# Score matmuls of a head pair in one batch, later side pieces, and a last gate strip finished by token tile

## The chip, the cores and the metric

The kernel runs on one core of a Trainium2 chip. The metric is the device time of one execution in microseconds (us), as the median of repeated runs. One further execution was recorded by the hardware profiler; every row below comes from that one.

## The reference

A two-layer encoder trunk over 256 tokens with a model width of 2048. Layer 0 mixes tokens by windowed grouped-query attention (32 query heads of 64, 4 key heads, a sink logit per head), layer 1 by differential attention (8 heads, each with two softmax maps of width 128). Each layer goes on with a gated feed-forward of width 5632 and with an embedding that is added through a gate.

```python
for i in range(DEPTH):
    hn = rms_norm(h, attn_norm[i])
    mix = windowed_gqa_sink(...) if i % 2 == 0 else diff_attention(...)
    h = h + mix
    h = h + swiglu(rms_norm(h, ffn_norm[i]), w_ffn_in[i], w_ffn_out[i])
    gate = sigmoid(rms_norm(h, ple_gate_norm[i]) @ ple_w_gate[i])
    h = h + rms_norm(p[i] @ ple_w_proj[i], ple_post_norm[i]) * gate

# layer 0: sc = q k^T * 64**-0.5 - slope * |t-s|, masked to |t-s| <= 128, softmax with the sink
# layer 1: sc = q k^T * 128**-0.5 - slope * |t-s|; probs[0] - lam * probs[1]; then v, rms_norm
```

## The kernel before

All 256 tokens stay on the chip as two token tiles (NM = 2) of 128. Every large product is cut into column strips of 512 (W). A strip is a `Group`: it runs over the contraction in steps k of 128 rows, and at each step over both token tiles, with three matmuls each, because both operands are held as a high and a low part (hi x hi, lo x hi, hi x lo). Such a matmul, 128x512 out, is called a strip matmul here (line 161 before, line 176 after, since the change shifts the lines). There are 9600 of them. The weights come by DMA into `raw`, and for every two steps k ScalarE (ACT) makes the high part `ws` and VectorE (DVE) the low part.

Everything else on TensorE (PE) is cut into side pieces, which are put between strip matmuls. PE's order is written by the kernel itself. `Flow` keeps a heap of pieces with due times on a clock `now`, which each strip matmul moves on by MM = 0.23. `flow.later(delay, fn)` enters a piece that is due `delay` after the present value of the clock; after each strip matmul `flow.tick` runs one step of the piece at hand, up to its next `yield`. So a piece that yields after each of its matmuls has a strip matmul between each two of them. Where a strip needs something that a piece has yet to make (`flow.until`), the pieces are run without strip matmuls in between; this is called a drain here. The order on ACT, DVE and GpSimd (POOL) is the scheduler's, and each of those engines works its list in that order.

The pieces of layer 0: `to_q` turns queries to columns by four transposes (line 386); `heads` makes the scores of two heads (line 396, helper `scores`) and sends them through `exps` (DVE `sc` and `nm`, ACT `e`, then POOL); `turn` transposes the weights of the two heads (line 425, eight transposes, then the splits `wT`); `weigh` multiplies them with the values (line 509, twelve matmuls, then the split of the result, `xt`). There are 16 head pairs. A score matmul of layer 0 contracts over 64 rows, one head on rows 0 to 63 and the other on rows 64 to 127 of the array. When one of the four strips of queries ends, `qk_norm` makes squares on ACT, sums `ss` on DVE, a reciprocal root in seven steps on POOL (its result is `rr`), and the normed queries `qn` on DVE.

Layer 1 has the same pieces with other sizes: the scores of a map are six matmuls over 128 rows, two maps for each of eight heads, and they read the keys and queries `qk` that `turn_side` splits on ACT and DVE just before. `Norm.turn` transposes the residual `h` (line 257) for the next product. All side pieces write into one pool of four buffers of the accumulation memory (`at`), taken in turn, so a piece waits until the fourth buffer back has been read.

The last strip of the whole program is the fourth gate strip of layer 1: after its last matmul, `gated` makes the sigmoid on ACT (line 727), two products and sums on DVE (lines 728 and 730), and one output DMA for each token tile (line 732).

Of the kernel before, what the change touches and what calls it, by code (L numbers as in the profile page):

```python
# [12 lines left out]
F32 = mybir.dt.float32  # L13
F32R = mybir.dt.float32r
AF = mybir.ActivationFunctionType
ALU = mybir.AluOpType
AX = mybir.AxisListType

P = 128
T = 256  # L20
NM = T // P
D = 2048
KT = D // P
W = 2 * T
SK = W // P
NS = D // W
# [9 lines left out]
MM = 0.23  # L36
# [49 lines left out]
def encoder(ctx: ExitStack, tc: tile.TileContext, x, p, attn_norm, ffn_norm, a_w_qkv, a_q_norm,  # L86
# [3 lines left out]
    nc = tc.nc  # L90
# [32 lines left out]
    def mslice(m):  # L123
        return slice(m * P, (m + 1) * P)
# [17 lines left out]
    class Group:  # L142


        def __init__(self, w, r0, n, c, xs, done, before=None):
            self.w, self.r0, self.n, self.c, self.xs, self.done, self.before = w, r0, n, c, xs, done, before
            self.blocks = [(b, min(4, n - b)) for b in range(0, n, 4)]

        def run(self, feed):
            if self.before:  # L150
                self.before()
            ps = [mm_ps() for _ in range(NM)]
            for k in range(self.n):
                if k % 2 == 0:
                    ws = feed.next()
                flow.until(lambda: len(self.xs) > k)
                x, hi, lo = self.xs[k], ws[:, 0, k % 2, :], ws[:, 1, k % 2, :]
                for m in range(NM):
                    c = mslice(m)
                    for i, (a, w) in enumerate(((0, hi), (1, hi), (0, lo))):  # L160
                        nc.tensor.matmul(ps[m], x[:, a, c], w, start=(k == 0 and i == 0),  # L161
                                         stop=(k == self.n - 1 and i == 2))
                        flow.tick(MM)
            self.ps = ps
            if self.done:
                self.done(ps)

    class Feed:

# [71 lines left out]
    class Norm:  # L241
# [2 lines left out]
        def __init__(self, col):  # L244
            self.col, self.stat, self.xs = col, Stat(), Slots()

        def add(self, s):
            self.stat.add([h[:, m, s * W:(s + 1) * W] for m in range(NM)])
            for k in range(s * SK, (s + 1) * SK, 2):
                flow.later(2.0, lambda k=k: self.turn(k))  # L250

        def turn(self, k):

# [136 lines left out]
    def scores(heads):  # L390

        for m in range(NM):
            c = mslice(m)
            for i, (a, b) in enumerate(((0, 1), (1, 0), (0, 0))):
                for ps, q, k in heads:
                    nc.tensor.matmul(ps[:, m, :], q[:, a, c], k[:, b, :], start=(i == 0), stop=(i == 2))  # L396
                yield 0.12 * len(heads)

    def exps(ps, d, slope, ap, extra=None):

# [40 lines left out]
    class AttentionA:  # L441
# [52 lines left out]
        def turn(self, j, es):  # L494
            wts = []
            for e in es:
                yield from keys_first(e, self.ap, WT_BUFS, wts)
                busy["e"] -= 1
            flow.later(2.0, lambda: self.weigh(j, wts))

        def weigh(self, j, wts):
            ps = at_ps()[:, 0, :]
# [19 lines left out]
    class AttentionB:  # L522
# [16 lines left out]
        def turn_side(self, hd, which, toks, b):  # L539
            s = self.hd.setdefault(hd, {"e": {}})  # L540
            t = self.ap.tile([P, 2, 2, T], F32R, name=f"qk{which}", tag=f"qk{which}", bufs=2)
            yield from to_pairs(t, toks, b * T, (gq_b, gk_b)[which])
            s[which] = t
            if which == 1:
                for c in range(2):
                    flow.later(2.0 + 2.0 * c, lambda c=c: self.scores(hd, c))

        def values(self, s):
            def done(ps):
# [81 lines left out]
    def project(w, os, norm):  # L631

        def done(half, s):
            def add(ps):
                add_to_h(ps, s)
                if half == 1:
                    norm.add(s)
            return add
        n = KT // 2

        class Half:
            def __len__(self):
                return max(0, len(os) - n)

            def __getitem__(self, k):
                return os[n + k]
        return [Group(w, half * n * P, n, s, (os, Half())[half], done(half, s))
                for half in range(2) for s in range(NS)]

    class FeedForward:  # L650
# [64 lines left out]
        def out(self, s, last):  # L715
            def done(ps):
                add_to_h(ps, s)
                if last:
                    self.gate.add(s)
            return done  # L720

        def gated(self, s, nxt):
            def done(ps):
                c = slice(s * W, (s + 1) * W)
                for m in range(NM):
                    g = self.fp.tile([P, W], F32, name="gate", tag="gate", bufs=2)
                    nc.scalar.activation(out=g, in_=ps[m], func=AF.Sigmoid, scale=self.gate.stat.col(m))
                    nc.vector.scalar_tensor_tensor(out=g, in0=g, scalar=self.pstat.col(m), in1=self.pe[:, m, c],  # L728
                                                   op0=ALU.mult, op1=ALU.mult)
                    nc.vector.tensor_tensor(out=h[:, m, c], in0=h[:, m, c], in1=g, op=ALU.add)  # L730
                    if nxt is None:
                        nc.sync.dma_start(out=out[mslice(m), c], in_=h[:, m, c])
                if nxt is not None:
                    nxt.add(s)
            return done

        def groups(self, nxt):
            lay, first, out, w_in = self.layer, 0, [], w_ffn_in[self.layer]
            for part in PARTS:
                last = first + part == FF // P  # L740
                hs = Slots()
                for i in range(part // SK):
                    s = first // SK + i
                    out.append(Group(w_in, 0, KT, s, self.norm.xs, self.gate_in))
                    out.append(Group(w_in, 0, KT, FF // W + s, self.norm.xs, self.up(hs, i * SK)))
                    if s < NS:
                        out.append(Group(ple_w_proj[lay], 0, 2, s, self.pp, self.embed(s)))
                for s in range(NS):
                    out.append(Group(w_ffn_out[lay], first * P, part, s, hs, self.out(s, last)))
                first += part  # L750
            out[0].before = self.start
            return out + [Group(ple_w_gate[lay], 0, KT, s, self.gate.xs, self.gated(s, nxt)) for s in range(NS)]

    attn_a = AttentionA(norm_a)
    norm = Norm(C_FFN)
# [25 lines left out]
    with tc.manual_schedule(engines={mybir.EngineType.Activation, mybir.EngineType.DVE}):  # L781
        for q in range(2):
            for _ in put_x(q):
                pass
        flow.later(6 * MM, lambda: put_x(2))
        flow.later(24 * MM, lambda: put_x(3))
        groups[0].done, first_done = None, groups[0].done
        groups[0].run(feed)
        for q in range(NS):
            feed.split()  # L790
            norm_a.stat.add([h[:, m, q * W:(q + 1) * W] for m in range(NM)])
    feed.ahead = WS_BUFS
    first_done(groups[0].ps)
    flow.later(3.0, small_vectors)
    for g in groups[1:]:
        g.run(feed)
# [53 lines left out]
```

## Time and profile before

| | us |
|---|---|
| median of 3 runs | 2399.95 |
| the 3 runs | 2399.94, 2399.95, 2404.16 |
| time of the profiled execution | 2401.06 |
| its span, first to last instruction | 2399.3 |
| PE busy in the span | 2367.5 |

The span is 1.8 us less than the time of that execution. Three views are read: the groups of instructions (busy time, count, mean), the timeline of an engine (start, length, what it waited for), and the sums over stretches. The end of a matmul is modelled in this profile, so what a matmul costs is read from start to start, not from its length. A bracket in a timeline row gives the idle time ahead of it and the engine that ended it.

### The profile page before, as it was taken

To read this page: it belongs to the slowest core of one execution; us is meant where nothing else is said; L and a number is where in the kernel's file an instruction comes from. 1 tells how busy PE (TensorE), PEld (TensorE's weight loads), DVE (VectorE), ACT (ScalarE), POOL (GpSimd) and SP (SyncE) were. 2 spreads that over 40 slices of the span, in tenths; PEclk is the share of its full clock that TensorE was granted. 3 is DMA by queue.
4 is the path that set the end of the run, shared out by engine and by line. 5 is a ranking of instruction groups with operands and counts; after the bars stand their busy time and mean duration, and the time that the engine had idled before them with its cause. 6 is when DMAs were issued, how large, how long until landed. Compare 5 with 4: busy or idle time off the path is not lost.

```text
span 2399.3 us, 28442 instructions
## 1 busy us (share of the span) xinstructions
PE 2367.5 (99%) x10853; PEld 1924.6 (80%) x10853; DVE 1345.4 (56%) x1546; ACT 1112.9 (46%) x1549; POOL 137.9 (6%) x309
## 2 busy tenths in 40 slices
PE   8999999999999999999999999999999999999998
PEld 6776788888888888887877888888888888888887
DVE  5667655555454454565557566655545554454564
ACT  5455454434434444455455454554444434434453
POOL 1232000000000000000111211000000000000000
PEclk9999999999999999999999999999999999999999
DMA  6432355555555555555544544555555555555553
GB/s 231 143 106 88 137 181 193 187 193 185 193 193 193 190 187 195 187 179 174 192 155 161 176 158 148 210 186 197 185 184 199 187 193 193 191 191 194 178 196 138
DMA packets 121281, 428.71 MB, mean 179 GB/s; under 512 B 13520, under 2 KB 16184, under 8 KB 120888
## 3 DMA queue, kind: packets, MB, share of 16 engines
q1 hardware_dynamic: 121144, 426.89, 51.0%
q8 instruction: 85, 1.39, 0.2%
q14 instruction: 52, 0.43, 0.0%
HBM read 424.74 MB, written 2.10 MB: 178 GB/s over the span
## 4 chain that ended last, share of the span: by engine, by line
PE 90%; DVE 2%; ACT 1%; issue 0%; POOL 0%; DVEq 0%; ACTq 0%; POOLq 0%
PE mm L161 86%; PE at L396 1%; PE at L708 1%; PE at L257 1%; DVE ws L139 1%; PE at L509 1%; PE at L595 0%; ACT ws L138 0%; PE at L425 0%; ACT e L411 0%; DVE gate L728 0%; PE at L386 0%; DVE qk L199 0%; DVE nm L407 0%; DVE sc L405 0%
## 5 line engine op out<-in xcount | busy, mean ns | idle before, releaser
L161 PE MATMUL mm<-ws,xt 128*128 128x512 f32 x9600 | 2324.8, 397 | 2.2 <-ACT xt L194 0.9
L161 PEld LDWEIGHTS mm<-ws,xt 128*128 128x128 f32 x9600 | 1790.1, 188 | 405.3 <-ACT xt L194 1.8
L139 DVE TENSOR_TENSOR ws<-raw,ws 128x1024 fp32r<-128x1024 f32 x800 | 978.1, 1226 | 875.5 <-ACT ws L138 875.0
L138 ACT CAST ws<-raw 128x1024 fp32r<-128x1024 f32 x800 | 840.6, 1052 | 1047.4 <-PE mm L161 958.8
L205 POOL TENSOR_SCALAR rs_v<-ssum 128x2 f32<-128x2 f32 x8 | 1.5, 193 | 1714.4 <-DVE ssum L234 1714.4
L286 DVE TENSOR_TENSOR h<-mm,h 128x512 f32<-128x512 f32 x96 | 62.0, 681 | 3.9 <-PE mm L161 3.9
L411 ACT ACTIVATE e<-sc,nm 128x257 f32<-128x257 f32 (+1 forms) x96 | 47.9, 501 | 34.6 <-DVE nm L407 34.3
L257 PE MATMUL at<-ident,h 128*128 128x128 f32 x192 | 52.7, 288 | 8.2 <-DMA h<-in_x_dram 6.0
L198 ACT ACTIVATE xt<-at,gains 128x256 fp32r<-128x256 f32 x96 | 43.2, 474 | 34.5 <-DVE xt L199 33.8
L194 ACT CAST xt<-at 128x256 fp32r<-128x256 f32 x108 | 37.9, 372 | 43.1 <-DVE xt L195 31.8
L199 DVE SCALAR_TENSOR_TENSOR xt<-at,gains,xt 128x256 fp32r<-128x256 f32 x96 | 44.1, 479 | 17.8 <-ACT xt L198 17.8
L195 DVE TENSOR_TENSOR xt<-at,xt 128x256 fp32r<-128x256 f32 x108 | 43.3, 418 | 15.6 <-ACT xt L194 15.3
L509 PE MATMUL at<-wT,vp 128*128 128x256 f32 x192 | 48.5, 291 | 2.8 <-DVE wT L195 2.0
L708 PE MATMUL at<-ident,hid 128*128 128x128 f32 x176 | 47.8, 272 | 0.0
L207 POOL TENSOR_TENSOR rs_y<-rs_v,halves 128x2 f32<-128x2 f32 (+2 forms) x29 | 44.8, 1546 | 2.4
L376 DVE TENSOR_TENSOR qn<-mm,rr 128x512 f32<-128x512 f32 (+1 forms) x28 | 16.9, 647 | 44.0 <-POOL rr L366 44.0
L425 PE MATMUL at<-ident,e 128*128 128x128 f32 x160 | 40.2, 272 | 0.8 <-DVE sc L405 0.8
L405 DVE SCALAR_TENSOR_TENSOR sc<-dist,at 128x512 f32<-128x512 f32 x48 | 31.5, 682 | 16.2 <-PE at L396 16.2
L689 ACT ACTIVATE silu<-mm,rinv 128x512 f32<-128x512 f32 x44 | 29.9, 688 | 19.7 <-PE mm L161 19.7
L257 PEld LDWEIGHTS at<-ident,h 128*128 128x128 f32 x192 | 27.7, 148 | 13.9 <-DMA h<-in_x_dram 6.6
L509 PEld LDWEIGHTS at<-wT,vp 128*128 128x128 f32 x192 | 34.2, 197 | 4.2 <-DVE wT L195 2.5
L396 PEld LDWEIGHTS at<-kd,qT 64*128 64x128 f32 x192 | 17.7, 183 | 24.3 <-issue 17.8
(90 smaller groups left out, 698.3 us busy)
## 6 DMA issues: line engine op xcount, KB each, us to landing
raw<-in_w_ffn_in_dram SPq DMA_DIRECT2D x352, 512.0 KB
raw<-in_w_ffn_out_dram SPq DMA_DIRECT2D x176, 512.0 KB
raw<-in_b_w_qkv_dram SPq DMA_DIRECT2D x96, 512.0 KB
raw<-in_ple_w_gate_dram SPq DMA_DIRECT2D x64, 512.0 KB
raw<-in_a_w_qkv_dram SPq DMA_DIRECT2D x40, 512.0 KB
raw<-in_a_w_o_dram SPq DMA_DIRECT2D x32, 512.0 KB
raw<-in_b_w_o_dram SPq DMA_DIRECT2D x32, 512.0 KB
raw<-in_ple_w_proj_dram SPq DMA_DIRECT2D x16, 256.0 KB
```

The lines of the kernel that those rows point to most:

```text
L138: nc.scalar.copy(out=ws[:, 0], in_=src)
L139: nc.vector.tensor_tensor(out=ws[:, 1], in0=src, in1=ws[:, 0].bitcast(F32), op=ALU.subtract)
L161: nc.tensor.matmul(ps[m], x[:, a, c], w, start=(k == 0 and i == 0), stop=(k == self.n - 1 and i == 2))
L195: nc.vector.tensor_tensor(out=lo, in0=src, in1=hi.bitcast(F32), op=ALU.subtract)
L198: nc.scalar.activation(out=hi, in_=src, func=AF.Copy, scale=scale)
L199: nc.vector.scalar_tensor_tensor(out=lo, in0=src, scalar=scale, in1=hi.bitcast(F32), op0=ALU.mult, op1=ALU.subtract)
L207: nc.gpsimd.tensor_tensor(out=y, in0=v, in1=halves[:, :n], op=ALU.pow)
L257: nc.tensor.transpose(ps[:, j, mslice(m)], h[:, m, (k + j) * P:(k + j + 1) * P], ident)
L286: nc.vector.tensor_tensor(out=hs, in0=ps[m], in1=hs, op=ALU.add)
L411: nc.scalar.activation(out=e[:, m, :], in_=sc[:, m, :], func=AF.Exp, bias=nm[:, m:m + 1], accum_out=den[:, m:m + 1])
L509: nc.tensor.matmul(ps, v[:, a, c0:c0 + P], wT[:, b, kh, :], start=(n == 0), stop=(n == 11))
L708: nc.tensor.transpose(ps[:, j, mslice(m)], hid[m][:, (j0 + j) * P:(j0 + j + 1) * P], ident)
```

## The change

The helper `scores` yields once at the end instead of after each of its six steps, so the twelve score matmuls of a head pair (layer 0), or the six of a map (layer 1), stand in a row. Several delays grow: `weigh` of layer 0 from 2.0 to 3.5, the scores of layer 1 from 2.0 to 4.5, the turning of `h` after the attention projection and after the feed-forward from 2.0 to 3.0, and after the gate of layer 0 from 2.0 to 5.0. The last gate strip runs its last four steps k by token tile: first all that is left of tile 0, then its end, then all of tile 1; and the end works in halves of 256 columns with an output DMA for each half.

```diff
-            for k in range(self.n):
+            apart = self.n - 4 if self.by_tile else self.n
+            for k in range(apart):
...
+            for k in range(apart, self.n, 2):
+                ws[k // 2] = feed.next()
+            for m in range(NM):
+                for k in range(apart, self.n):
+                    self.tile(ps, k, m, ws[k // 2])
+                self.done(ps, m)
...
-                flow.later(2.0, lambda k=k: self.turn(k))
+                flow.later(delay, lambda k=k: self.turn(k))
...
                 for ps, q, k in heads:
                     nc.tensor.matmul(ps[:, m, :], q[:, a, c], k[:, b, :], start=(i == 0), stop=(i == 2))
-                yield 0.12 * len(heads)
+        yield 1.0
...
-            flow.later(2.0, lambda: self.weigh(j, wts))
+            flow.later(3.5, lambda: self.weigh(j, wts))
...
-                    flow.later(2.0 + 2.0 * c, lambda c=c: self.scores(hd, c))
+                    flow.later(4.5 + 2.0 * c, lambda c=c: self.scores(hd, c))
...
-                    norm.add(s)
+                    norm.add(s, 3.0)
...
-                    self.gate.add(s)
+                    self.gate.add(s, 3.0)
...
-                    nxt.add(s)
+                    nxt.add(s, 5.0)
...
+        def gated_last(self, ps, m):
+            for i in range(2):
+                c, c0 = slice(i * T, (i + 1) * T), D - W + i * T
+                hs = h[:, m, c0:c0 + T]
+                g = self.fp.tile([P, W], F32, name="gate", tag="gate", bufs=2)[:, :T]
+                nc.scalar.activation(out=g, in_=ps[m][:, c], func=AF.Sigmoid, scale=self.gate.stat.col(m))
+                nc.vector.scalar_tensor_tensor(out=g, in0=g, scalar=self.pstat.col(m), in1=self.pe[:, m, c0:c0 + T],
+                                               op0=ALU.mult, op1=ALU.mult)
+                nc.vector.tensor_tensor(out=hs, in0=hs, in1=g, op=ALU.add)
+                nc.sync.dma_start(out=out[mslice(m), c0:c0 + T], in_=hs)
...
+            if nxt is None:
+                out[-1].by_tile, out[-1].done = True, self.gated_last
```

On PE, at the first head pair of layer 0: `mm` is a strip matmul, `at<-ident,qn` a transpose of the queries, `at<-kd,qT` a score matmul. Before (the pattern of two scores and one strip matmul goes on, six times in all):

```order
L386 MATMUL at<-ident,qn 128x128
L161 MATMUL mm<-ws,xt 128x512 x10
L396 MATMUL at<-kd_435,qT 128x256 x2
L161 MATMUL mm<-ws,xt 128x512
L396 MATMUL at<-kd_435,qT 128x256 x2
...
L396 MATMUL at<-kd_435,qT 128x256 x2
L161 MATMUL mm<-ws,xt 128x512 x9
L386 MATMUL at<-ident,qn 128x128
```

The same place on PE after the change:

```order
L398 MATMUL at<-ident,qn 128x128
L176 MATMUL mm<-ws,xt 128x512 x10
L408 MATMUL at<-kd_435,qT 128x256 x12
L176 MATMUL mm<-ws,xt 128x512 x16
L398 MATMUL at<-ident,qn 128x128
```

The five strip matmuls that stood between the pairs now stand behind the batch.

On PE, at the first head of layer 1 (`at<-qk,qk` is a score matmul there, and the transposes ahead of it make the keys that it reads). Before:

```order
L386 MATMUL at<-ident,qn 128x128
L161 MATMUL mm<-ws,xt 128x512 x10
L396 MATMUL at<-qk_9146,qk_8973 128x256
L161 MATMUL mm<-ws,xt 128x512
L396 MATMUL at<-qk_9146,qk_8973 128x256
```

After:

```order
L398 MATMUL at<-ident,qn 128x128
L176 MATMUL mm<-ws,xt 128x512 x21
L408 MATMUL at<-qk_9146,qk_8973 128x256 x6
L176 MATMUL mm<-ws,xt 128x512 x4
L408 MATMUL at<-qk_9146,qk_8973 128x256 x6
```

There are 21 strip matmuls between the transposes and the first score where there were 10, and the six scores of a map stand together.

On DVE, at the end of the third strip of queries in layer 0 (`ss` and `qn` belong to `qk_norm`; `xt` is the split of the result of a `weigh`, which frees its `at` buffer; `sc` reads the scores). Before:

```order
L363 TENSOR_REDUCE ss_1195<-sq_1196 128x8
L195 TENSOR_TENSOR xt_1187<-at_1159,xt_1187 128x256
L363 TENSOR_REDUCE ss_1195<-sq_1199 128x8
L139 TENSOR_TENSOR ws_1220<-raw_935,ws_1220 128x1024
L376 TENSOR_TENSOR qn_1214<-mm_841,rr_1212 128x512
L376 TENSOR_TENSOR qn_1216<-mm_842,rr_1212 128x512
L405 SCALAR_TENSOR_TENSOR sc_1242<-dist_107,at_1191 128x2x256
```

After:

```order
L375 TENSOR_REDUCE ss_1238<-sq_1239 128x8
L426 RECIPROCAL rd_1195<-den_1191 128x2
L426 RECIPROCAL rd_1208<-den_1204 128x2
L375 TENSOR_REDUCE ss_1238<-sq_1242 128x8
L139 TENSOR_TENSOR ws_1263<-raw_975,ws_1263 128x1024
L388 TENSOR_TENSOR qn_1257<-mm_841,rr_1255 128x512
L388 TENSOR_TENSOR qn_1259<-mm_842,rr_1255 128x512
L207 TENSOR_TENSOR xt_1282<-at_1226,xt_1282 128x256
```

The split of a `weigh` result, which stood between the two sums, now stands behind `qn`, which waits for POOL.

## Rows read from the trace of the kernel before

**Rows 1.** Page: an engine's busy time; groups with busy us, mean ns, idle.

```profile
PE 2367.5 (99%) x10853; PEld 1924.6 (80%) x10853; DVE 1345.4 (56%) x1546; ACT 1112.9 (46%) x1549; POOL 137.9 (6%) x309
L161 PE MATMUL mm<-ws,xt 128*128 128x512 f32 x9600 | 2324.8, 397 | 2.2 <-ACT xt L194 0.9
L396 PEld LDWEIGHTS at<-kd,qT 64*128 64x128 f32 x192 | 17.7, 183 | 24.3 <-issue 17.8
```

**Rows 2.** Chain of waits in order of time (start us, us, what), one undisturbed piece.

```profile
368.56 44.48 PE mm L161 x196
```

**Rows 3.** PE timeline (start us, length us), one run of layer 0 scores.

```profile
217.33 0.39 PE L396 MATMUL at<-kd,qT 64*128 64x256 f32 x2
217.65 0.49 PE L161 MATMUL mm<-ws,xt 128*128 128x512 f32 x1
218.07 0.39 PE L396 MATMUL at<-kd,qT 64*128 64x256 f32 x2
...
221.06 0.38 PE L396 MATMUL at<-kd,qT 64*128 64x256 f32 x2
221.37 0.98 PE L161 MATMUL mm<-ws,xt 128*128 128x512 f32 x3
```

**Rows 4.** PE timeline in the first drain of layer 0.

```profile
195.82 0.98 PE L396 MATMUL at<-kd,qT 64*128 64x256 f32 x11 [0.19 <-DVE xt L195]
196.73 1.68 PE L509 MATMUL at<-wT,vp 128*128 128x256 f32 x12
198.87 0.50 PE L161 MATMUL mm<-ws,xt 128*128 128x512 f32 x1 [0.46 <-ACT xt L194]
199.88 0.50 PE L161 MATMUL mm<-ws,xt 128*128 128x512 f32 x1 [0.51 <-DVE xt L195]
```

**Rows 5.** PE timeline at a first score of layer 1.

```profile
1297.54 2.54 PE L161 MATMUL mm<-ws,xt 128*128 128x512 f32 x10
1300.73 0.39 PE L396 MATMUL at<-qk,qk 128*128 128x256 f32 x1 [0.65 <-DVE qk L199]
...
1301.19 0.28 PE L396 MATMUL at<-qk,qk 128*128 128x256 f32 x1
...
1301.54 0.29 PE L396 MATMUL at<-qk,qk 128*128 128x256 f32 x1
```

**Rows 6.** Who PE waited for: us in total, times, longest us.

```profile
PE at L396 <- DVE qk L199: 7.8, 8, 2.8
PE at L257 <- DVE h L730: 2.2, 4, 1.5
```

**Rows 7.** Sums over stretches: busy us of PE, PEld, DVE, ACT, POOL; clock; DMA.

```profile
1231.80:1235.10 3.30, 3.30 (x11) 2.77 (x11) 2.59 (x5) 0.60 (x2) 0.00 (x0) 0.50 0.25 68
79.70:279.90 200.20, 193.56 (x989) 138.48 (x988) 133.77 (x211) 100.85 (x227) 53.85 (x115) 0.99 0.31 109
```

**Rows 8.** PE timeline at the first transposes of `h` after the gate of layer 0.

```profile
1085.76 1.75 PE L161 MATMUL mm<-ws,xt 128*128 128x512 f32 x7
1089.05 0.30 PE L257 MATMUL at<-ident,h 128*128 128x128 f32 x1 [1.54 <-DVE h L730]
```

**Rows 9.** DVE timeline after the end of the second strip of queries.

```profile
97.42 1.29 DVE L376 TENSOR_TENSOR qn<-mm,rr 128x512 f32<-128x512 f32 x2 [4.30 <-POOL rr L366]
98.62 1.28 DVE L405 SCALAR_TENSOR_TENSOR sc<-dist,at 128x512 f32<-128x512 f32 x2
```

**Rows 10.** PE timeline, the third run of layer 0 scores.

```profile
99.42 0.91 PE L396 MATMUL at<-kd,qT 64*128 64x256 f32 x2
```

**Rows 11.** Timeline of the end of the program: ACT, DVE and the DMA queue.

```profile
2392.63 1.37 ACT L727 ACTIVATE gate<-mm,rinv 128x512 f32<-128x512 f32 x2 [9.15 <-PE mm L161]
2393.35 1.43 DVE L728 SCALAR_TENSOR_TENSOR gate<-gate,rinv,pe 128x512 f32<-128x512 f32 x2 [8.61 <-ACT gate L727]
2394.70 1.28 DVE L730 TENSOR_TENSOR h<-h,gate 128x512 f32<-128x512 f32 x2
2395.41 0.93 SPq L732 DMA_DIRECT2D out_dram<-h  x2
```

More of the change, by code (lines that the diff above doesn't have):

```diff
@@ L146, in __init__ @@
             self.w, self.r0, self.n, self.c, self.xs, self.done, self.before = w, r0, n, c, xs, done, before
+            self.by_tile = False
             self.blocks = [(b, min(4, n - b)) for b in range(0, n, 4)]
@@ L152, in run, with tile @@
             ps = [mm_ps() for _ in range(NM)]
-            for k in range(self.n):
+            apart = self.n - 4 if self.by_tile else self.n
+            ws = {}
+            for k in range(apart):
                 if k % 2 == 0:
-                    ws = feed.next()
+                    ws[k // 2] = feed.next()
                 flow.until(lambda: len(self.xs) > k)
-                x, hi, lo = self.xs[k], ws[:, 0, k % 2, :], ws[:, 1, k % 2, :]
                 for m in range(NM):
[L159 to L166, printed above, removed]
+                    self.tile(ps, k, m, ws[k // 2])
+            if not self.by_tile:
+                if self.done:
+                    self.done(ps)
+                return ps
+            for k in range(apart, self.n, 2):
+                ws[k // 2] = feed.next()
+            for m in range(NM):
+                for k in range(apart, self.n):
+                    self.tile(ps, k, m, ws[k // 2])
+                self.done(ps, m)
+        def tile(self, ps, k, m, ws):
+            x, hi, lo = self.xs[k], ws[:, 0, k % 2, :], ws[:, 1, k % 2, :]
+            for i, (a, w) in enumerate(((0, hi), (1, hi), (0, lo))):
+                nc.tensor.matmul(ps[m], x[:, a, mslice(m)], w, start=(k == 0 and i == 0),
+                                 stop=(k == self.n - 1 and i == 2))
+                flow.tick(MM)
     class Feed:
@@ L245, in __init__, with add @@
             self.col, self.stat, self.xs = col, Stat(), Slots()
-        def add(self, s):
+        def add(self, s, delay):
             self.stat.add([h[:, m, s * W:(s + 1) * W] for m in range(NM)])
             for k in range(s * SK, (s + 1) * SK, 2):
-                flow.later(2.0, lambda k=k: self.turn(k))
+                flow.later(delay, lambda k=k: self.turn(k))
         def turn(self, k):
@@ L751, in groups @@
             out[0].before = self.start
-            return out + [Group(ple_w_gate[lay], 0, KT, s, self.gate.xs, self.gated(s, nxt)) for s in range(NS)]
+            out += [Group(ple_w_gate[lay], 0, KT, s, self.gate.xs, self.gated(s, nxt)) for s in range(NS)]
+            if nxt is None:
+                out[-1].by_tile, out[-1].done = True, self.gated_last
+            return out
     attn_a = AttentionA(norm_a)
@@ L787, in encoder @@
         groups[0].done, first_done = None, groups[0].done
-        groups[0].run(feed)
+        first_ps = groups[0].run(feed)
         for q in range(NS):
@@ L792, in encoder @@
     feed.ahead = WS_BUFS
-    first_done(groups[0].ps)
+    first_done(first_ps)
     flow.later(3.0, small_vectors)
```

## The prediction

> **What bounds the kernel now.** I read the busy times first, then the groups, then the timeline of PE, and at last the sums over stretches. PE is busy for 2367.5 of 2399.3 us, the next engine, DVE, for 56% of the span [rows 1]. The strip matmuls alone hold 2324.8 us of that, and they wait for almost nothing (2.2 us idle) [rows 1]. An undisturbed piece of 196 of them takes 44.48 us, so one costs 0.227 us from start to start [rows 2]; 9600 of them are 2179 us. The change leaves every one of them in place. What it can win is in the other 220 us: the side pieces, at whatever they cost between strip matmuls, and the waits of PE. So each step below is a sum on PE, from start to start, and the question behind it is whether DVE, ACT and POOL keep up when PE comes round sooner.
>
> **Scores of layer 0: minus 25.4 us.** In the run of rows 3 the six pairs go from 217.33 to 221.37, which is 4.04 us, with five strip matmuls in it; less 5 x 0.227 that is 2.9 us for 12 small matmuls. Each step costs 0.74 us for a pair and a strip matmul (217.33 to 218.07), so a pair costs 0.52 [rows 3]. The two heads of a pair work on different halves of the rows, and each change between such a pair and a full strip matmul costs time. In the drain the trace already holds what the change writes everywhere: from the second score matmul at 195.82 (the first had started just before the stall) to the next piece at 196.73 all six pairs take 0.91 us [rows 4]. The exit there goes to another small matmul; into a strip matmul it takes up to 0.1 more (0.31 us, from 221.06 to 221.37, rows 3). I take 1.0 for a batch, so a batch saves 2.9 - 1.0 = 1.9 us. Of 16 runs in the timeline 13 look like rows 3, one is half in the drain, and two stand wholly in it and win nothing. 13 x 1.9 + 0.7 = 25.4 us, all of it on PE, which sets the end. Bounds: 24 (exit 0.1 dearer) and 27 (exit as in the drain).
>
> **Scores of layer 1: minus 11.6 us.** Here a score matmul costs 0.35 us together with its strip matmul (1301.19 to 1301.54, rows 5), so 0.12 by itself, about what 256 columns cost at half the time of a strip matmul. Standing in a row they can't get much cheaper; I take zero. The gain is the delay. Before, the first score stands ten strip matmuls behind the transposes; they would end at 1297.54 + 2.27 = 1299.81, and the score starts at 1300.73, because DVE is still at the low part of the keys [rows 5]. The row shows 0.65 us idle and 0.92 are lost from start to start, the rest being the pipeline that fills again. There are 8 such waits with 7.8 us idle, the longest 2.8 [rows 6]; with 8 x 0.27 for the refill that is 10.0 us. The change puts 21 strip matmuls there instead of 10, thus 2.5 us more cover against waits of 0.9; against the longest, 2.8, stand these 2.5 us and a new order on DVE, in which the split of the keys no longer comes behind the last steps of the second map's softmax. All eight go. Behind the longest wait the clock is granted at 0.50, 1.2 GHz instead of 2.4, for the 3.3 us of a row in which PE runs 11 matmuls [rows 7]; half of that, 1.6 us, goes too. What is late next is the transposed weight of the first head of a pair, now only two strip matmuls behind the second head's scores; the product with the values follows 17 strip matmuls later, 3.9 us, as before. I charge nothing, and up to 3 us in the range.
>
> **Turning `h` after the gate: minus 3.0 us.** Seven strip matmuls from 1085.76 end at 1087.35, the transpose starts at 1089.05, behind the sum on DVE: 1.7 us [rows 8]. Four such waits have 2.2 us idle [rows 6], and about 0.2 each for the refill. The delay moves the transposes 13 strip matmuls back, 2.9 us, more than the longest wait. Their splits on ACT and DVE are needed 42 strip matmuls after the last transpose, so nothing is late. The same move by five strip matmuls at the three other places meets no wait in the trace and is worth zero.
>
> **The last strip: minus 1.1 us.** The number of strip matmuls is the same. Token tile 0 ends 12 strip matmuls (2.7 us) sooner and its end is covered by them. For tile 1 the chain now is: ACT from 2393.31 (the second of the two in the row), two products, two sums, the last DMA issued at 2396.0 [rows 11]: 2.7 us. In halves it is one half of an ACT pass (0.34) and four DVE passes of half the length (2 x 0.36 + 2 x 0.32 = 1.36), and some 0.2 for hand-overs: 1.9. With 0.3 us for a DMA of half the size that is 1.1; bounds 0.5 and 1.6. There are two more passes on ACT, four on DVE and two DMAs, all within this.
>
> **What is given back in layer 0: plus 6 us.** PE now runs the stretch from 79.7 to 279.9 in some 25 us less, but DVE has the same 133.8 us of work in it [rows 7]: 67% before, 76% after. That alone is no bound. The order is: at the end of a strip of queries DVE stands for 4.30 us until POOL has the root, and only then comes `sc`, which frees an `at` buffer [rows 9]. The third run of scores waited for that already, and its first pair takes 0.91 us where others take 0.39 [rows 10]. Between the end of that strip and this run PE had 25 strip matmuls, a run of scores and eight transposes, 5.7 + 2.9 + 0.9 = 9.5 us, and waited about 0.5. Now it has 22, a batch and the same transposes, 5.0 + 1.0 + 0.9 = 6.9 us. DVE is free perhaps 0.5 sooner, so PE waits 9.5 + 0.5 - 0.5 - 6.9 = 2.6, say 3 us. At the end of the third strip the new order puts the split of a `weigh` result behind the same wait (about 8.9 us after the strip's end, 4.3 of it POOL), and the scores that need its buffer come 5.7 us after: 3 us more. The fourth strip is followed by two `weigh` pieces that use older buffers; zero. Each 3 us wait may bring a slow stretch as that of 2.8 us did, 1.6 us each. Against this the first drain shrinks from eight pieces in chain to five, and one of its three waits of about 1 us stays. The whole of layer 0 shows 200.2 - 193.6 = 6.6 us of PE idle [rows 7], with refill and a slow stretch some 10 us. After: 3 + 3 + 3 for the slow stretches, 4 in the drain, 1.5 at each of two forced ends (as the two waits at 198.87 and 199.88 in rows 4, which come to 1.0 of idle), 16 in all. That is 6 more. Bounds: minus 4, if earlier work on DVE frees it in time, and plus 18, if the other batches wait some 1 us each as well. Delaying `weigh` by 6 strip matmuls only helps here. Nothing queues behind the moved pieces on the DMA queue: its order changes in the output DMAs alone.
>
> **The sum.** -25.4 - 11.6 - 3.0 - 1.1 + 6 = -35.1 us. The profiled execution took 2401.06, 1.1 above the median of the runs; it gives 2366, and against the median I predict 2365 us.
>
> **Rivals.** *Nothing is given back:* DVE's shorter work ahead of `qk_norm` covers both places. Then 2400 - 41 = 2359. For it speaks that before a run of scores there waited no longer than the half microsecond of rows 10.
>
> *DVE paces layer 0:* batch after batch waits for the fourth buffer back. With 1 us for each of 16 on top it is 2365 + 16 = 2381. Against it stands the 76% share, for it that one engine's stand of 4.3 us has no slack left. The Trainium skill, TensorEngine Tiling (Array Packing), section PSUM Bottleneck, warns of just this: tiling makes TensorE faster but not the emptying of the accumulators, which may become the bottleneck. No row shows it at full length.
>
> *A batch is dearer than in the drain:* the weight load of the next pair doesn't hide behind the matmuls of the pair ahead. Then a pair costs a load of 0.183 us [rows 1] and half a strip matmul, 0.11, so a batch 6 x 0.29 + 0.2 = 1.95; it saves 0.95 and the layer 13, and the time is 2377. The Trainium skill, TensorE: Matmul & The Clock Gate, section The mechanism, says that a weight load overlaps with matmuls in flight only where the row groups differ, which here holds within a pair and not from pair to pair. The trace speaks against that price: 0.91 for six pairs [rows 4].
>
> *Slower:* the waits in layer 0 are long enough for a slow clock each time. A wait of 3 us and 1.6 us behind it at 12 batches are 55 us, 2365 + 55 - 7.6 for the two places counted already: 2412. It turns slower from a mean of 2.6 us per batch (41 / 16). Only the two places of `qk_norm` show such a length.
>
> **Chances.** Forecast 0.50 (2360 to 2372), nothing given back 0.20, DVE paces 0.17, dearer batch 0.07, slower 0.04, within 0.2% (about 5 us, what a measurement of this kernel can tell from no change) 0.02. Faster is the sum of the first four, 0.94. The range 2353 to 2382 takes in the bounds of the batch, the delay and the give-back, and leaves out the ends of the rivals.
>
> **What would show it.** Twelve scores in about 1.0 us, and strip matmuls on either side. No wait of scores for `qk` on DVE in layer 1 and no slow clock there; none for `h` on DVE. Waits for DVE at the scores behind the second and third strip of queries, of about 3 us. An end of some 4.9 us after the last strip matmul where it took 6.0. I am wrong if the batch takes 2 us, if DVE's share in layer 0 nears 90%, or if the clock is low for more than two stretches there.

## The result and the profile after

The changed kernel takes 2368.96 us (median of four runs, 2368.39 to 2369.39) where the kernel before takes 2402.05 (four runs, 2399.94 to 2405.84): a ratio of 0.986, 95% interval 0.9843 to 0.9877. The forecast was 2365.0. The profiled execution took 2368.39 us with a span of 2366.6, against 2399.3 before: 32.7 us less.

The strip matmuls are the same 9600 in the same order, so they serve as mile posts: the time from the start of one to the start of another is compared between two traces, whatever was moved in between. This table is worked out from the PE timelines in that way, in us. Each column is one profiled execution; where the same code stands in several traces, layer 0 of the changed kernel takes 188.8 to 190.7 us (three traces) and layer 1 of the kernel before 335.4 to 336.8 (three traces), so a difference of 1 to 2 us in a layer tells nothing.

| strip matmuls, counted from 0 | what lies there | before | after less before | forecast |
|---|---|---|---|---|
| 255 to 725 | attention of layer 0 | 205.6 | -16.2 | -19.4 |
| 4180 to 4500 | behind the gate of layer 0 | 80.2 | -3.7 | -3.0 |
| 4500 to 5760 | attention of layer 1 | 336.8 | -10.7 | -11.6 |
| last strip matmul to the end of the span | last strip | 6.4 | -0.9 | -1.1 |
| up to the first strip matmul | the input lands | 12.8 | -1.1 | 0 |
| all the rest | | 1757.4 | -0.1 | 0 |

The page of after first: PE's busy time (2367.5 before, rows 1), and its strip matmuls, whose idle time before them has grown from 2.2 us to 6.1.

```profile
PE 2339.1 (99%) x10853; PEld 1920.7 (81%) x10853; DVE 1345.3 (57%) x1550; ACT 1117.6 (47%) x1551; POOL 138.6 (6%) x309
...
L176 PE MATMUL mm<-ws,xt 128*128 128x512 f32 x9600 | 2302.8, 397 | 6.1 <-DVE xt L207 4.2
```

A run of layer 0 scores in after, on the PE timeline (start us, length us). It answers to [rows 3]: twelve matmuls stand in one row, and from the strip matmul ahead of them to the one behind them it is 1.00 us more than a strip matmul's own 0.227; before, the same difference was 3.00.

```profile
202.23 0.71 PE L176 MATMUL mm<-ws,xt 128*128 128x512 f32 x2
202.87 0.97 PE L408 MATMUL at<-kd,qT 64*128 64x256 f32 x12
203.77 0.96 PE L176 MATMUL mm<-ws,xt 128*128 128x512 f32 x3
```

The first scores of layer 1, answering to [rows 5]: 21 strip matmuls in place of ten, then six scores in 0.71 us (1284.51 to 1285.22), no idle time noted at them.

```profile
1279.63 5.05 PE L176 MATMUL mm<-ws,xt 128*128 128x512 f32 x21
1284.51 0.87 PE L408 MATMUL at<-qk,qk 128*128 128x256 f32 x6
1285.22 1.09 PE L176 MATMUL mm<-ws,xt 128*128 128x512 f32 x4
```

Whom PE waited for in after (us in total, times, longest us). Against [rows 6], the waits for `qk` and for `h` on DVE are gone; in their place stand waits for `xt` and `sc` on DVE, and all of them lie in layer 0.

```profile
PE at L408 <- DVE xt L207: 4.5, 1, 4.5
PE mm L176 <- DVE xt L207: 4.2, 3, 2.6
PE at L408 <- DVE sc L417: 2.6, 2, 2.4
```

Three of them are long, and each of the three stands behind the same thing. At the end of the second, third and fourth strip of queries DVE's next instruction is the scaling of the strip, `qn`, and DVE stands there for 4.58, 4.58 and 4.62 us until POOL has computed the inverse root `rr`. What PE wants comes behind it: at the second strip `sc`, which frees a buffer of the scores; at the third `xt` of a weighted sum, which frees the buffer for the second head's scores; at the fourth two `xt` with a split of weights between them. There PE is 31 matmuls into the first strip of the output product, whose operands the `xt` are, and it goes on when the second of the two is done (180.30 and 0.41). DVE and PE at the three places (start us, length us, and in brackets the idle time before it and who ended it):

```profile
94.14 1.29 DVE L388 TENSOR_TENSOR qn<-mm,rr 128x512 f32<-128x512 f32 x2 [4.58 <-POOL rr L378]
95.34 1.28 DVE L417 SCALAR_TENSOR_TENSOR sc<-dist,at 128x512 f32<-128x512 f32 x2
96.08 0.38 PE L408 MATMUL at<-kd,qT 64*128 64x256 f32 x1 [2.35 <-DVE sc L417]
...
133.89 1.29 DVE L388 TENSOR_TENSOR qn<-mm,rr 128x512 f32<-128x512 f32 x2 [4.58 <-POOL rr L378]
135.09 0.41 DVE L207 TENSOR_TENSOR xt<-at,xt 128x256 fp32r<-128x256 f32 x1
135.56 1.65 PE L408 MATMUL at<-kd,qT 64*128 64x256 f32 x11 [4.46 <-DVE xt L207]
...
177.63 1.29 DVE L388 TENSOR_TENSOR qn<-mm,rr 128x512 f32<-128x512 f32 x2 [4.62 <-POOL rr L378]
178.84 0.41 DVE L207 TENSOR_TENSOR xt<-at,xt 128x256 fp32r<-128x256 f32 x1
179.17 1.21 DVE L139 TENSOR_TENSOR ws<-raw,ws 128x1024 fp32r<-128x1024 f32 x1
180.30 0.41 DVE L207 TENSOR_TENSOR xt<-at,xt 128x256 fp32r<-128x256 f32 x1
180.77 0.50 PE L176 MATMUL mm<-ws,xt 128*128 128x512 f32 x1 [2.65 <-DVE xt L207]
```

At the first two the granted clock falls to 0.50, that is 1.2 GHz in place of 2.4, for 3.4 and 6.8 us: 1.7 us after PE has gone on at the first, and 0.3 us before it goes on at the second. The sums over these two stretches (busy us of PE, PEld, DVE, ACT, POOL; clock; DMA share; GB/s) show 9 and 26 matmuls that run in them; layer 1 has no such stretch left [rows 7].

```profile
97.74:101.16 3.42, 3.42 (x9) 2.65 (x10) 3.20 (x8) 3.07 (x10) 2.49 (x6) 0.50 0.00 0
135.29:142.12 6.83, 6.55 (x26) 5.03 (x27) 5.18 (x9) 1.32 (x2) 0.00 (x0) 0.50 0.00 0
```

### The profile page after: what moved, and what is told of

Same layout as the page of the kernel before. It is cut to its first block, busy times and chain, and to the rows that moved or that the text cites. A ratio compares the mean times of both kernels' runs of the same rounds, so it can differ in the third digit from the quotient of the medians.

```text
span 2366.6 us, 28473 instructions
## 1 busy us (share of the span) xinstructions
PE 2339.1 (99%) x10853; PEld 1920.7 (81%) x10853; DVE 1345.3 (57%) x1550; ACT 1117.6 (47%) x1551; POOL 138.6 (6%) x309
## 4 chain that ended last, share of the span: by engine, by line
PE 96%; DVE 1%; DMA 1%; POOL 1%; ACT 1%; issue 1%; SPq 0%; DVEq 0%; ACTq 0%; POOLq 0%
PE mm L176 91%; PE at L408 1%; PE at L720 1%; PE at L269 1%; DMA h<-in_x_dram 1%; PE at L521 1%; PE at L437 1%; PE at L607 1%; PE at L398 0%; DVE ws L139 0%; POOL rs_y L219 0%; ACT ws L138 0%; DVE sc L417 0%; DMA raw<-in_a_w_qkv_dram 0%; DVE nm L419 0%
## 5 line engine op out<-in xcount | busy, mean ns | idle before, releaser
L501 POOL TENSOR_SCALAR e<-e,rd 128x256 f32<-128x256 f32 x64 | 33.6, 538 | 14.0 <-DVE rd L426 12.4
L206 ACT CAST wT<-at 128x512 fp32r<-128x512 f32 x40 | 22.9, 580 | 23.5 <-PE at L437 23.4
```

The source lines that it names most:

```text
L206: nc.scalar.copy(out=hi, in_=src)
```

## The experiments

The ratios compare with the kernel before on the same chip. "Layer 0" and "layer 1" are the stretches of the table above in one profiled execution, and a difference without another word is to the kernel before. The runs lie on several chips; the two long stretches that no edit touches take 802.6 to 802.7 and 889.6 to 889.7 us in all of them, so times of different runs may be compared too.

### Which part wins what

**The changed kernel without the batch** (the score runs give way after every step again, all the delays stay):

```
                     nc.tensor.matmul(ps[:, m, :], q[:, a, c], k[:, b, :], start=(i == 0), stop=(i == 2))
-        yield 1.0
+                yield 0.12 * len(heads)
```

> The changed kernel with the scores yielding after each step again, all delays and the last strip as changed. Theory (a batch saves the changes between half-row pairs and full strip matmuls; PE then runs into DVE, which stands for POOL): a run of layer 0 scores costs 3.0 us again instead of 1.0 (13 runs, 26 us lost), and the waits of 3.0, 5.2 and 2.9 us behind the strips of queries and the two slow stretches there shrink to under 1 us together with them (10 to 12 us won back). Net 2369 + 15 = 2384 us (2380 to 2388); layer 1 keeps its gain, no wait of scores for the keys. Rival (the longer delays made the gain of layer 0): 2369 to 2373.

2400.32 us (2397.28 to 2408.71), ratio 0.9999 (0.9988 to 1.001), far from both 2384 and the rival's 2369 to 2373: the delays by themselves win nothing. The gate won its 3.7 us. Layer 1 won only 4.8: four of the eight waits for `qk` stay, at the scores of every second head (4.9 us idle). And layer 0 became 10.2 us longer than before, which I had not expected at all. It has two stretches at half clock, of 6.8 and 10.2 us, where the kernel before had one of 3.4. At half speed the additional 13.7 us cost some 7 of the 10.2. Here they are as sums over stretches:

```profile
144.00:150.80 6.80, 6.80 (x20) 4.53 (x20) 3.73 (x6) 1.78 (x3) 0.00 (x0) 0.50 0.39 146
188.30:198.60 10.30, 10.30 (x42) 7.32 (x42) 4.64 (x7) 2.77 (x5) 0.00 (x0) 0.50 0.23 91
```

**The kernel before with the batch alone:**

```
                     nc.tensor.matmul(ps[:, m, :], q[:, a, c], k[:, b, :], start=(i == 0), stop=(i == 2))
-                yield 0.12 * len(heads)
+        yield 1.0
```

> The kernel before with the batched scores alone. Theory: layer 0 gains some 16 us net, as in the changed kernel; layer 1 keeps its eight waits for the keys (8 us idle or more, since the scores come no later) and the slow stretch behind the longest, the wait for h after the gate stays at 2.2 us idle, the end stays 6.4 us. 2400 - 16 = 2384 us. Rival (the batch itself removes the waits of layer 1, because DVE gets its scores sooner): 2372.

2390.14 us, ratio 0.9956 (0.9941 to 0.9971). That is 6 us more than expected. In layer 0 the batch alone brings 15.9 us, as much as the whole change. In layer 1 it does harm: 7.0 us longer, the same eight waits with 13.5 us idle where there were 7.8 [rows 6]. From the list of PE's waits in this run:

```profile
PE at L396 <- DVE qk L199: 13.5, 8, 2.7
```

**The changed kernel with layer 1's delay back at 2.0**, the batch kept. It sets my account of layer 1 (the delay everything, the batch nothing) against the run just told:

```
-                    flow.later(4.5 + 2.0 * c, lambda c=c: self.scores(hd, c))
+                    flow.later(2.0 + 2.0 * c, lambda c=c: self.scores(hd, c))
```

> The changed kernel with the delay ahead of layer 1's scores back at 2.0, the batch kept. As the prediction has it (the batch is worth nothing in layer 1, the delay everything): layer 1 as in the kernel before, 10.7 us longer than in the changed kernel, 2380 us (2378 to 2382). Theory from the run with the batch alone (layer 1 got 7.0 us longer there, since a batch spends the time ahead of it without strip matmuls): layer 1 17.7 us longer than in the changed kernel, 8 waits for qk with some 13.5 us, 2387 us (2385 to 2389).

2389.59 us, ratio 0.9939 (0.9919 to 0.9958): 20.6 us more than the changed kernel, and in the profiled execution layer 1 is 11.1 us longer than in the kernel before, 21.8 longer than in the changed one. The account of the prediction (2380) falls, and the time lies just above the 2385 to 2389 of the other. The timelines show how the batch does harm without the delay. PE at the first two heads of layer 1 in this run, and DVE ahead of the second:

```profile
1278.44 2.54 PE L176 MATMUL mm<-ws,xt 128*128 128x512 f32 x10
1281.64 0.97 PE L408 MATMUL at<-qk,qk 128*128 128x256 f32 x6 [0.65 <-DVE qk L211]
1282.45 1.32 PE L176 MATMUL mm<-ws,xt 128*128 128x512 f32 x5
1283.61 0.88 PE L408 MATMUL at<-qk,qk 128*128 128x256 f32 x6
...
1286.78 2.54 PE L176 MATMUL mm<-ws,xt 128*128 128x512 f32 x10
1292.05 1.65 PE L408 MATMUL at<-qk,qk 128*128 128x256 f32 x6 [2.73 <-DVE qk L211]
...
1289.10 1.09 DVE L584 SCALAR_TENSOR_TENSOR e<-e,rd 128x256 f32<-128x256 f32 x2 [0.71 <-POOL e L582]
1290.12 1.21 DVE L139 TENSOR_TENSOR ws<-raw,ws 128x1024 fp32r<-128x1024 f32 x1
1291.25 0.74 DVE L211 SCALAR_TENSOR_TENSOR qk<-at,cols,qk 128x512 fp32r<-128x512 f32 x1
```

The first wait is as before, 0.65 us. The second head's turn comes sooner, and in DVE's queue the product `e` of the first head's softmax, which stands 0.71 us for POOL, and a split of weights now go ahead of the `qk` that PE wants. In the kernel before, the same `qk` started at 1309.10, ahead of that `e` (1309.82), and PE waited 0.79 us there. The wait becomes 2.73 us, and from just before its end the clock is at half (1291.4 to 1298.3). The eight waits are those of the run with the batch alone, 13.5 us idle in both; that this layer 1 is 4 us longer still goes with the clock, which is at half for 17.1 us of it and for 6.8 us there. In layer 1 neither edit is worth its share by itself: delay alone -4.8, batch alone +7.0 to +11.1, both -10.7.

**The kernel before with only the delay ahead of layer 0's weighted sums** raised, to see whether that is what made the run without the batch lose 10 us:

```
-            flow.later(2.0, lambda: self.weigh(j, wts))
+            flow.later(3.5, lambda: self.weigh(j, wts))
```

> The kernel before with the one delay ahead of the weighted sums of layer 0 raised from 2.0 to 3.5, scores still in single steps. Theory from the run without the batch, whose layer 0 took 10.2 us more than before: this delay is what costs that, because steps pushed back meet the next head's steps and TensorE stands at them and loses its clock: layer 0 8 to 12 us longer, all else as before: 2411 us (2408 to 2414). Rival (the 10 us came from the delays elsewhere or from another order of the pieces): layer 0 within 3 us of before, 2402 us.

2407.3 us, ratio 1.0027 (1.0015 to 1.0038): slower, with layer 0 6.8 us longer and the rest as before. That is below the 8 to 12 I had given. Set against the 10.2 it is two thirds, half of it (some 3.4 us) again half clock, 10.2 us of it in place of 3.4; the other delays were not tried by themselves. Some of it is seen at the end of the layer, in a row of the PE timeline and the sum over the stretch behind it: PE comes to a weighted sum whose transposed weights DVE hasn't split yet, waits 2.48 us, and runs at half clock.

```profile
270.67 2.43 PE L509 MATMUL at<-wT,vp 128*128 128x256 f32 x12 [2.48 <-DVE wT L195]
...
271.40:274.60 3.20, 2.74 (x11) 2.19 (x10) 2.42 (x6) 1.46 (x6) 0.00 (x0) 0.50 0.00 0
```

**The changed kernel with the last strip in one piece again:**

```
-                out[-1].by_tile, out[-1].done = True, self.gated_last
+                pass
```

> The changed kernel with the last gate strip finished as before, in one piece for both token tiles. Theory: only the end changes, the last strip matmul to the end of the span takes 6.4 us again in place of 5.5: 2370 us (2369 to 2371). Rival (the earlier first store takes nothing off, the 0.9 us are chance): 2369 us with 5.5 us at the end.

2369.65 us, ratio 0.987 (0.9853 to 0.9886). From the start of the last strip matmul to the end of the span it is 6.41 us again (6.40 before, 5.51 after), and the gate and both layers are as in the changed kernel to 0.7 us. Over all traces the end takes 6.4 us where the strip is in one piece and 5.5 to 5.7 where it is not. So 0.7 to 0.9 us are the strip's, though a difference of 0.7 in the medians is no more than the runs spread.

### What is given back in layer 0

**Two blocks of six in place of one batch of twelve**, with one strip matmul between the blocks:

```
                     nc.tensor.matmul(ps[:, m, :], q[:, a, c], k[:, b, :], start=(i == 0), stop=(i == 2))
-        yield 1.0
+            yield 0.5
```

> The changed kernel with a yield after each half of the scores, so that a run of layer 0 stands in two blocks of six matmuls with a strip matmul between. Theory (the price is that of a change between half-row pairs and full strips): six blocks cost 3.0 us, one costs 1.0, so 0.4 for each further block, and two cost 1.4; 16 runs make 6 us, less 1 to 2 that the waits behind get shorter: 2373 us (2370 to 2376). Rival (a pair is cheap only behind many others): a run costs about 2 us and the time is 2380 or more.

2368.68 us, ratio 0.9865 (0.985 to 0.9879), the same as the changed kernel. An undisturbed run costs 1.40 us as expected, 0.4 more than a batch; over some ten runs that is 4 us more on PE, and layer 0 is still -16.2, where I expected 2373 us in all. PE's waits in layer 0 shrank from 14.7 to 8.4 us, while its time at half clock grew from 10.2 to 13.7. So PE's own price no longer set layer 0: something else did.

**The scaling entered later:** the changed kernel, with VectorE's scaling of a strip of queries put into the program 7.0 later than the root.

```
-    def qk_norm(srcs, rinv, nh, dh, dup, qp):
+    def qk_norm(srcs, rinv, nh, dh, dup, qp, wait=0.0):
...
+        def scale():
...
+        if wait:
+            flow.later(wait, scale)
+        else:
+            scale()
...
-                toks = qk_norm(ps, self.norm.stat.r, W // A_DH, A_DH, False, self.ap)
+                toks = qk_norm(ps, self.norm.stat.r, W // A_DH, A_DH, False, self.ap, 7.0)
```

> The changed kernel with the two multiplications qn of each strip of queries of layer 0 entered 7.0 on the clock after the sums, so that DVE does other work while POOL makes the root; nothing else moves, DVE's total work is the same. Theory (what is given back in layer 0 is DVE standing 4.6 us for POOL): the waits of 3.0, 5.2 and 2.9 us and the slow stretches behind the first two (10 us of half clock, 5 us lost) go or fall under 1 us each; 2369 - 13 = 2356 us (2352 to 2360). Rival (DVE's total share in layer 0, 77%, paces PE): the waits move to other scores and the time stays within 3 us of 2369.

2364.21 us, ratio 0.9846 (0.983 to 0.9863): -21.6 in layer 0, 4.8 better than the changed kernel where I expected 13. The wait behind the second strip went. At the third and fourth the scheduler that orders DVE's instructions had put the scaling early again, and DVE stood nearly as long as before; PE waited 3.86 and 2.98 us there, and 10.2 us of layer 0 are at half clock as in the changed kernel. DVE's timeline in this run:

```profile
130.91 0.69 DVE L389 TENSOR_TENSOR qn<-mm,rr 128x512 f32<-128x512 f32 x1 [4.24 <-POOL rr L378]
...
175.50 1.29 DVE L389 TENSOR_TENSOR qn<-mm,rr 128x512 f32<-128x512 f32 x2 [4.30 <-POOL rr L378]
```

So this run left the question open: DVE's standing, or its load?

**The scaling on GpSimd:** the changed kernel, in which DVE only copies the strip out of PSUM and POOL, which has the root, multiplies. DVE's list has the same number of instructions as in the changed kernel, and `sc` and the `xt` that PE had waited for stand at the same places of it; the copies stand up to three places ahead of where the scalings stood, and the wait for POOL is gone.

```
-            for c in range(rep):
+            if dh == A_DH and not dup:
+                nc.vector.tensor_copy(out=q[:, :n], in_=srcs[m])
+                nc.gpsimd.tensor_tensor(out=q4[:, :, 0, :], in0=q4[:, :, 0, :],
+                                        in1=rr[:, m, :].unsqueeze(2).broadcast_to([P, nh, dh]), op=ALU.mult)
+            for c in range(0 if dh == A_DH and not dup else rep):
```

> The changed kernel, with one edit for the query strips of layer 0: VectorE only copies a strip out of PSUM (it waits for nothing of GpSimd any more), and GpSimd, which computes the inverse root, multiplies the copy by it. VectorE's order and its number of instructions are the same as in the changed kernel. Theory (VectorE standing 4.6 us behind each of three roots is what is left of layer 0's loss): the three waits of 3.0, 5.1 and 2.9 us and the half-speed stretches of 10.2 us behind them (5 us) go, 16 us less in layer 0, nothing elsewhere: 2353 us (2350 to 2358). Rival (the work of VectorE is too dense there anyway, and the waits return elsewhere, as they did by half when the scaling was only entered later): 2364 us (2361 to 2369). Second rival (GpSimd's multiplications of 128x512 come too late for the transposes of the strip): waits of TensorE for GpSimd at the transposes of qn, 2366 us or more.

2355.18 us (2354.57 to 2355.43), ratio 0.9809 (0.9795 to 0.9824): the fastest of all, 13.8 us below the changed kernel. Layer 0 is 31.0 us shorter than before, 14.8 shorter than after the change, and everything else is as in the changed kernel. The timelines of DVE and POOL at the second strip of queries in this run:

```profile
89.96 1.28 DVE L388 COPY qn<-mm 128x512 f32<-128x512 f32 x2
91.16 1.22 DVE L139 TENSOR_TENSOR ws<-raw,ws 128x1024 fp32r<-128x1024 f32 x1
92.29 1.28 DVE L421 SCALAR_TENSOR_TENSOR sc<-dist,at 128x512 f32<-128x512 f32 x2
...
90.42 2.91 POOL L219 TENSOR_TENSOR rs_y<-rs_v,halves 128x16 f32<-128x16 f32 x1
...
94.61 0.22 POOL L378 TENSOR_TENSOR rr<-rs_r,rinv 128x16 f32<-128x16 f32 x1
94.90 2.91 POOL L389 TENSOR_TENSOR qn<-qn,rr 128x512 f32<-128x512 f32 x2
```

DVE reaches `sc` at 92.29 where it reached it at 95.34, though this trace is 1.7 us later than that of after at this place, and the run of scores behind it, from 95.41, costs 1.01 us with no wait. POOL's two multiplications take 1.45 us each and PE waits nowhere for them. No stretch of layer 0 is at half clock, with DVE busy for 135.12 of 175.00 us, 77%; in the changed kernel the same layer held 135.2 us of its work. The sum over it in this run:

```profile
78.00:253.00 175.00, 169.66 (x1013) 135.97 (x1013) 135.12 (x213) 103.94 (x230) 62.01 (x121) 1.00 0.37 128
```

This settles the question: it was the standing, not the load.

The Trainium skill, GPSIMD Engine Reference, section Specifications, says that GpSimd has no access to PSUM; that is why DVE makes the copy here, and no run here shows what would happen otherwise.

**The same edit on the kernel before.** If the standing was a cost all along, this wins as much; if the batch uncovered it, next to nothing.

> The kernel before, scores still in single steps, with the one edit that took 14 us off the changed kernel: VectorE copies a query strip of layer 0 out of PSUM and GpSimd scales it. Theory (before the change VectorE's stand of 4.3 us was hidden by the dear score steps, and became a cost only with the batches): TensorE's waits for VectorE in layer 0 were some 5 us in all and none longer than 1.1 us, so at most 3 us are won: 2399 us (2396 to 2402). Rival (the stand cost the kernel before as much, spread over small waits): layer 0 10 us or more shorter, 2390 us or less.

2398.44 us, ratio 0.9982 (0.9973 to 0.9991), 4.3 us by the medians, layer 0 3.1 us shorter. Of the 3.1, 1.2 lie at two runs of scores, which cost 3.00 us each here and 3.53 and 3.70 before, and some 1.7 are a stretch at half clock (190.7 to 194.1 before) that this execution does not have. The edit that is worth 14.8 us behind the batch is worth 3 to 4 without it.

## Why the prediction was right, and where it was off

**The batch of layer 0: right, a little too small.** I took 1.9 us a run, from one row of the drain [rows 4]. The runs show 3.00 before and 1.00 after, 2.0: 13 x 2.0 + 0.7 = 26.7 us instead of 25.4. The row of the drain was the right one to read: what the same instructions cost when they happen to stand together. The rival of the dearer batch (1.95 us) falls by the rows at 202.87. The rule behind that rival, the Trainium skill, TensorE: Matmul & The Clock Gate, section The mechanism, has weight loads overlap only where the row groups differ; here six pairs that alternate the two halves take 0.90 us, so any loss from pair to pair is small in these rows.

**What is given back in layer 0: right mechanism, mis-sized term.** I had +6; the layer won 16.2 of 26.7, so 10.5 came back. My +6 was +9 (two waits of 3 us, and 3 for slow stretches) and -3 (the rest of layer 0 waiting 7 us where it waited 10). The run with the scaling on GpSimd takes the first apart from the second: without the standing layer 0 wins 31.0, so the standing costs 14.8 and not 9, and the rest gives 4.3 and not 3. The 14.8 by places: at the second strip 3.0, as I had it; at the third a run of scores costs 6.5 in place of 1.0, 5.5 where I had 3; at the fourth PE starts 2.9 late, where I had zero; and the half clock, 10.2 us at half speed, costs some 5, of which 0.7 lie in the 5.5 already. That makes 15.8 by the rows, against 14.8 by the run.

The step that failed is the one for the fourth strip. I argued that two weighted sums with older buffers follow it, and looked at the buffers alone. But those sums' results are operands of the output strip that PE was in, and their splits `xt` (178.84 and 180.30) stood behind `qn` as well. At the third strip I took 8.9 us from the strip's end to the `xt` and 5.7 to the scores. It was 11.6 (first square at 123.89, `xt` done at 135.50) and 6.8 (130.73), so 4.8 in place of 3.2, and the 0.7 of the half clock come on top. The `xt` was late because the second square, which POOL's root needs, stood behind four exponentials in ACT's queue; at the second strip the two squares stood together.

```profile
123.89 0.69 ACT L374 ACTIVATE sq<-mm,rinv 128x512 f32<-128x512 f32 x1 [0.47 <-PE mm L176]
...
126.44 0.67 ACT L374 ACTIVATE sq<-mm,rinv 128x512 f32<-128x512 f32 x1
```

**Layer 1: right sum, wrong split.** -10.7 against -11.6, and what I said would be seen is there: no wait for `qk`, no half clock, 0.118 us a score. But that the gain is the delay and the batch is worth zero is wrong by the runs, and that the sum came out is in part luck: the change made both edits at once. The delay alone wins 4.8, since at every second head a wait stays; the batch alone costs 7.0. I priced the batch by what it takes on PE, and that is zero indeed; what it does to the distance between one head's scores and the next head's I left out. Had the change been the batch alone, the same reasoning would have promised 19 us (25.4 less the 6 given back), and the run won 11.

**The gate and the end:** -3.7 against -3.0, and -0.9 against -1.1. The end takes 5.1 us from the end of the last strip matmul, where I named 4.9 and it took 6.0. The last instructions of after, which answer to [rows 11], are half as wide but take some 0.6 of the time (0.84 for 1.37, 0.88 for 1.43, 0.75 for 1.28), where I reckoned with half:

```profile
2361.52 0.84 ACT L755 ACTIVATE gate<-mm,rinv 128x256 f32<-128x256 f32 x2 [1.88 <-PE mm L176]
2362.03 0.88 DVE L756 SCALAR_TENSOR_TENSOR gate<-gate,rinv,pe 128x256 f32<-128x256 f32 x2 [1.17 <-ACT gate L755]
2362.82 0.75 DVE L758 TENSOR_TENSOR h<-h,gate 128x256 f32<-128x256 f32 x2
```

**The delay of `weigh`,** of which I said that it only helps: not shown to help. With the batch the delay makes no difference in layer 0 (-15.9 with the old delays, -16.2 with the new), and without it it costs 6.8 us.

**The rivals.** "Nothing is given back" said 2359; it needs the standing gone, and the run in which it is gone gives 2355. "DVE paces layer 0" is refuted in its form (a wait at every batch), since ten undisturbed runs cost 1.00 us and DVE's share was 72% in after and 77% in the fastest version. The Trainium skill, TensorEngine Tiling (Array Packing), section PSUM Bottleneck, warns that emptying PSUM may become the bottleneck once TensorE is faster; so it did at two of the three places (at the fourth strip PE lacked an operand), but by a stand in DVE's queue and not by its throughput.

1.1 us of the 32.7 are not the change's: the first strip matmul started earlier because the input landed earlier in that execution; over all traces it starts between 11.7 and 12.8 us.

## What to carry to other kernels

Price a step that moves by what the same instructions cost where the trace already has them in that arrangement, and then ask of every engine that feeds it not how busy it is but what it stands for. An engine that waits in its queue for a slower one delays whatever is queued behind, for whomever; as long as PE comes round late nobody sees it. When a batch or a faster step uncovers such a stand, move the waiting instruction to the engine that it waits for: here that was worth 14 us behind the batch, and 3 to 4 before it. And of two edits that meet at one place, measure both apart and together: here one alone loses, the other wins half.

## What the runs showed of the hardware

Two matmuls on different halves of the rows cost 0.50 us as a pair between strip matmuls and 0.15 in a row of six pairs (0.90 us); one more change over to strip matmuls and back costs 0.4 us (1.40 for two blocks against 1.00 for one). Six scores over all rows, 256 columns each, cost 0.71 us in a row and 0.12 each between strip matmuls, so for them the arrangement makes no difference.

In the changed kernel stretches at half clock, of 3.4 and 6.8 us, came with stalls of TensorE of 2.35 and 4.46 us, and none with one of 2.65 us. The same stall can go either way: at the second head of layer 1, 2.79 us brought 3.4 us at half clock in the kernel before and none in the kernel before with the scaling on GpSimd; of four stalls of 2.7 us in layer 1, two brought a stretch in the run with the batch alone, and all four did in the run with layer 1's delay put back. These traces don't tell which stalls bring one.

GpSimd took 2.91 us for the power in the root of a query strip (128x16, line 219) and 1.45 us for a product of 128x512, so the power of a small tile takes as long as two large products.
